# Heads in pairs on half-array tiles, and modulation slices in four column groups, in a two-layer diffusion trunk on Trainium2

## The chip, the cores and the metric

The program runs on one core of a Trainium2 chip. The metric is the device time of one execution in microseconds (us). The engines are PE (TensorE, matrix products), DVE (VectorE), ACT (ScalarE), POOL (GpSimd, here the indirect gathers) and SP (SyncE, which issues most DMAs). Each engine works off its own queue in a fixed order; semaphores tie the queues together.

## The reference

640 tokens (128 context tokens, group i; 512 latent tokens, group ii) of width 1024 pass two layers. A layer, cut to what matters here:

```python
sh1, sc1, g1, sh2, sc2, g2 = modulate(cvec, w_ada, b_ada)      # silu(c) @ w_ada + b_ada, 6 x 1024 per group
h = rmsnorm(x) * (1 + sc1) + sh1
qa, ka, va, ga, lrf, lrb, ch, cb, cc, qn, kn, vn = split_proj(h, w_in)
o_gla = gla_bidir(q, k, v, la_f, la_b, s0_f, s0_b)             # 6 heads of 64, both directions, chunked scan with decay
y_conv = cb * short_conv(cc * ch, conv_w, conv_b)              # 256 channels
o_na = neighbourhood_attention(qh, kh, vh, ...)                # 6 heads of 64, softmax(q k^T * scale + bias) v
x = x + g1 * (concat(y_gla, y_conv, o_na) @ w_out)
x = x + g2 * peer_ffn(rmsnorm(x) * (1 + sc2) + sh2, ...)       # product-key retrieval of 128 single-neuron experts
```

All products are float32 in result: the projections split each operand into a rounded part and its rest and add three products, the others are float32 matrix products as such.

## The kernel before

Channels lie on the 128 partitions, tokens along the free dimension (`T` = 640, five chunks of 128). Two heads of 64 channels share a partition block, so linear attention (GLA) and neighbourhood attention (NA) loop over three blocks `fc`, each a pair of heads: partitions 0 to 63 are one head, 64 to 127 the other.

**Modulation.** `w_ada` of a layer is 12 slices of 512 outputs, each 8 blocks of 128x512. `ada_steps` loads a block (256 KB, `wada`), multiplies it by the two conditioning columns `sc` (L160, `ps_ada`, 8 matmuls added up in one PSUM bank), copies the two rows out (L165, `arow`) and turns them to columns by four small matmuls (L172, `ps_at`). It is a generator: layer 0 takes slices 0 to 2 on PE and slice 3 on DVE (L158) ahead of everything else, slices 4 to 9 two blocks at a time between the head steps of its NA, and slices 10, 11 and layer 1's twelve during the retrieval front end of layer 0. Layer 1 computes none.

**Projections.** A chunk of 128 output channels (`proj`, L221) loads a 512 KB weight block, splits it (`whi` on ACT L217, `wlo` on DVE L218) and issues 48 matmuls (L233, `ps_pj`), 8 blocks of the width by 3 products by 2 halves of 320 tokens.

**GLA.** `pre(fc)` makes the decays (`dec`, a chain of `ps_z`, DVE `mz` and three ACT functions) and four projection chunks (192 matmuls): q, k, v, gate. `gla(fc)` computes the diagonal products `ps_d` (L339, contraction over one head's 64 partitions), and then seven levels of a doubling scheme: 20 records of `ps_lv` matmuls (L361; a float32 matmul leaves two records, and ten stand in a level), whose results go into `att` under a mask (L362, `copy_predicated`), after which `qz` (L375) and `kS` (L377) are scaled for the next level. `qz` is stored twice as wide, with zeros in the other head's half, so that one matmul over all 128 partitions gives both heads. A tail transposes `kS`, chains six state steps (`pk` L404 on PE, `st` L407 on DVE) and forms the output `po` (L419 from the states, L423 from `att`), which is normalised and gated. `pre(fc+1)` is emitted behind `gla(fc)`.

**NA.** `na(fc)` runs five query tiles for one head and then five for the other: scores `ps_s` (L506, L508), bias and row maximum on DVE (L511), exponential on ACT (L516), scaling on DVE (L518), transposes (L522, `pt`), a copy out (L524, `pT`), and the products with the values into 64 of 128 partitions (L527, `npo`). `napre(fc+1)` has three more projection chunks.

**Then** the output projection (8 chunks), and the retrieval layer: norm, query projections and top-k (`level1`, `select`), one-hot tables (`build`), then a loop over 128 rows of experts that holds PE, DVE, POOL and the DMA queues.

**Order.** The code emits instructions in program order, and a scheduler gives each engine one fixed order from it: work emitted later may be put ahead where the engine would otherwise stand idle by the scheduler's reckoning. So `pre(fc+1)`'s matmuls can stand between the levels of `gla(fc)`. What stands where is read from the order of the built program.

Of the kernel before, what the change touches and what calls it, by code (L numbers as in the profile page):

```python
# [42 lines left out]
CG = ((0, 1), (1, 5))  # L43
TG = 256
# [9 lines left out]
NADA = 2  # L54
# [4 lines left out]
ADAP = 3  # L59
ORDER = "b2 s3 b3 s4 l0 b4 s0".split()  # L60
BSEL = 16
ADA1 = 4
NWA = 4
# [6 lines left out]
class Trunk:  # L70
    def __init__(self, ctx, tc, I, O):
# [21 lines left out]
        self.sc = consts.tile([128, 8, 2], F32, name="sc")  # L93
        with tc.tile_pool(name="init", bufs=1) as ip:
            for name, shape, dst, dt in (("cT", [128, 8, 2], None, F32), ("lmask", [128, 7, 128], self.lmask, I32),
                                         ("thr", [128, 2, 16], self.thr, F32), ("nstep", [128, 16], self.nstep, F32),
                                         ("iota", [128, 128], self.iota, F32)):
                t = ip.tile(shape, dt, name="i_" + name)
                nc.scalar.dma_start(t, I[name])
                if dst is None:  # L100
                    S.activation(self.sc, t, AF.Silu)
                else:
                    V.tensor_copy(dst, t)
        self.eps = consts.tile([128, 1], F32, name="eps")
# [36 lines left out]
    def ada_steps(self, l, c0, c1, dve=False):  # L141
        nc, PE, S, V = self.nc, self.PE, self.S, self.V
        for m in range(c0, c1):
            pt = None
            if dve:
                part = self.wp.tile([128, 2, 512], F32, name="apart", tag="apart", bufs=1)
            else:
                ps = self.pss.tile([128, 512], F32, name="ps_ada", tag="s")
            for k in range(8):
                w = self.wp.tile([128, 512], F32, name="wada", tag="wadv" if dve else "wada", bufs=2 if dve else NWA)  # L150
                nc.sync.dma_start(w, self.I["w_ada"][l, m, k])
                if dve:
                    for g in range(2):
                        c = self.sc[:, k, g:g + 1]
                        if k == 0:
                            V.tensor_scalar(part[:, g, :], w, c, None, op0=OP.mult)
                        else:
                            V.scalar_tensor_tensor(part[:, g, :], w, c, part[:, g, :], op0=OP.mult, op1=OP.add)  # L158
                else:
                    PE.matmul(ps[0:2, :], self.sc[:, k, :], w, start=(k == 0), stop=(k == 7))  # L160
                if k < 7:
                    yield
            if not dve:
                row = self.adap.tile([2, 512], F32, name="arow", tag="arow")
                S.activation(row, ps[0:2, :], AF.Copy)  # L165
            pt = self.pss.tile([128, 4, 2], F32, name="ps_at", tag="s")
            for i in range(4):
                if dve:
                    for g in range(2):
                        PE.matmul(pt[:, i, g:g + 1], part[:, g, i * 128:(i + 1) * 128], self.one, start=True, stop=True)  # L170
                else:
                    PE.matmul(pt[:, i, :], row[:, i * 128:(i + 1) * 128], self.ident[0:2, 0:2], start=True, stop=True)  # L172
# [64 lines left out]
    def mix(self, l):  # L237
# [21 lines left out]
        first = chain.from_iterable(zip_longest(self.ada_steps(l, 0, ADAP), self.ada_steps(l, ADAP, 4, True))) if l == 0 else ()  # L259
# [23 lines left out]
        qz = [gp.tile([128, 2, T], F32, name=f"qz{d}") for d in range(2)]  # L283
        sts = [gp.tile([128, 4, 128], F32, name=f"st{d}") for d in range(2)]
        for d in range(2):
            for hh in range(2):
                r = slice(64 * hh, 64 * hh + 64)
                o = slice(64 - 64 * hh, 128 - 64 * hh)
                G.memset(qz[d][r, 1 - hh, :], 0.0)
# [32 lines left out]
        def gla(fc, X):  # L322
# [3 lines left out]
            for d in range(2):  # L326
                for hh in range(2):
                    r = slice(64 * hh, 64 * hh + 64)
                    V.tensor_tensor(qz[d][r, hh, :], q[r, :], dec[d][r, :], op=OP.mult)
            att = gp.tile([128, 5, 2, 128], F32, name="att", tag="att")  # L330
            PAIRS = ((0, 1), (1, 3), (3, 5))
            for c0, c1 in PAIRS:
                n = c1 - c0
                pd = [pss.tile([128, 2, 128], F32, name="ps_d", tag="s") for hh in range(2)]
                for hh in range(2):
                    r = slice(64 * hh, 64 * hh + 64)
                    for c in range(c0, c1):
                        cs = slice(c * 128, c * 128 + 128)
                        PE.matmul(pd[hh][:, c - c0, :], kS[0][r, cs], q[r, cs], start=True, stop=True)  # L339
                    V.scalar_tensor_tensor(att[:, c0:c1, hh, :], pd[hh][:, :n, :], 2.0,  # L340
                                           ident[:, None, :].to_broadcast([128, n, 128]), op0=OP.mult, op1=OP.mult)
            tot = dec
            for lb in range(7):
# [7 lines left out]

                for c0, c1 in PAIRS:
                    n = c1 - c0
                    ps = pss.tile([128, 2, 2, 128], F32, name="ps_lv", tag="s")
                    for c in range(c0, c1):
                        cs = slice(c * 128, c * 128 + 128)
                        for d in range(2):
                            z = 1 - d
                            o = ps[:, c - c0].rearrange("p h (n z b) -> p h n z b", z=2, b=b)[:, :, :, z, :]
                            x = qz[d][:, :, cs].rearrange("p h (n z b) -> p h n z b", z=2, b=b)[:, :, :, z, :]  # L360
                            PE.matmul(o, kS[d][:, cs], x, start=True, stop=True)  # L361
                    V.copy_predicated(att[:, c0:c1].rearrange("p c h t -> p (c h) t"),  # L362
                                      self.lmask[:, lb, None, :].to_broadcast([128, 2 * n, 128]),
                                      ps[:, :n].rearrange("p c h t -> p (c h) t"))
                nb = T // (2 * b)
                tv = [tot[d].rearrange("p (n z) -> p n z", z=2) for d in range(2)]
                for d in range(2):
                    z = 1 - d
                    qv = qz[d].rearrange("p h (n z b) -> p (h n) z b", z=2, b=b)[:, :, z, :]
                    if b == 1:  # L370
                        qv = qv[:, :, 0].rearrange("p (h n) -> p h n", h=2)
                        V.tensor_tensor(qv, qv, tv[d][:, None, :, d].to_broadcast([128, 2, nb]), op=OP.mult)
                    else:
                        qv = qv.rearrange("p (h n) b -> p h n b", h=2)
                        V.tensor_tensor(qv, qv, tv[d][:, None, :, d:d + 1].to_broadcast([128, 2, nb, b]), op=OP.mult)  # L375
# [34 lines left out]
            for g, (c0, c1) in enumerate(CG):  # L410
                n = c1 - c0
                po = pss.tile([128, 4, 128], F32, name="po", tag="s")
                for c in range(n):
                    cs = slice((c + c0) * 128, (c + c0 + 1) * 128)
                    first = True
                    if g:
                        for d in range(2):
                            for hh in range(2):
                                PE.matmul(po[:, c, :], qz[d][:, hh, cs], sts[d][:, c, :], start=first, stop=False)  # L419
                                first = False  # L420
                    for hh in range(2):
                        r = slice(64 * hh, 64 * hh + 64)
                        PE.matmul(po[:, c, r], att[:, c0 + c, hh, :], vt[:, c0 + c, r], start=not g,  # L423
# [61 lines left out]
        def na(fc, Y):  # L485
            q, k, vt = Y["q"], Y["k"], Y["vt"]
            po = [pss.tile([128, 4, 128], F32, name="npo", tag=f"o{i}", bufs=1) for i in range(2)]
            for hh in range(2):
                r = slice(64 * hh, 64 * hh + 64)
                bt = np_.tile([128, BW], F32, name="bt", tag="bt", bufs=2)  # L490
                nc.sync.dma_start(bt, I["bias"][l, 2 * fc + hh])
                for qt in range(5):
                    ps = pss.tile([128, 512], F32, name="ps_s", tag="s")
                    qs = slice(qt * 128, qt * 128 + 128)
                    s = np_.tile([128, 512], F32, name="ss", tag="ss", bufs=3)
                    mx = np_.tile([128, 4], F32, name="mx", tag="mx", bufs=4)
                    if qt == 0:
                        N = 128
                        PE.matmul(ps[:, :128], q[r, qs], k[r, :128], start=True, stop=True)
                        vs = [vt[:, 0, r]]  # L500
                        V.tensor_reduce(mx[:, 0:1], ps[:, :N], axis=AX.X, op=OP.max)
                        src = ps
                    else:
                        kt0, kn = NAK[qt - 1]
                        N = (kn + 1) * 128
                        PE.matmul(ps[:, :kn * 128], q[r, qs], k[r, (1 + kt0) * 128:(1 + kt0 + kn) * 128],  # L506
                                  start=True, stop=True)
                        PE.matmul(ps[:, kn * 128:N], q[r, qs], ck[r, fc, :], start=True, stop=True)  # L508
                        vs = [vt[:, 1 + kt0 + i, r] for i in range(kn)] + \
                             [cv[:, fc * 128 + 64 * hh:fc * 128 + 64 * hh + 64]]  # L510
                        V.tensor_tensor_reduce(out=s[:, :N], in0=ps[:, :N],  # L511
                                               in1=bt[:, BOFF[qt - 1][0]:BOFF[qt - 1][0] + N], scale=1.0,
# [7 lines left out]
                    nk = N // 128  # L520
                    for i in range(nk):
                        PE.transpose(pt[:, i, :], s[:, i * 128:(i + 1) * 128], ident)  # L522
                    pT = np_.tile([128, 4, 128], F32, name="pT", tag="pT", bufs=2)
                    S.activation(pT[:, :nk, :], pt[:, :nk, :], AF.Copy)  # L524
                    o = po[0][r, 0, :] if qt == 0 else po[1][r, qt - 1, :]
                    for i in range(nk):
# [43 lines left out]
    def peer(self, l):  # L570
# [55 lines left out]
        for h in range(PH):  # L626
# [10 lines left out]
            for _ in range(ADA1):  # L637
                next(ada, None)
# [369 lines left out]
```

## Time and profile before

| | us |
|---|---|
| median of 3 runs | 4127.65 (4120.05 to 4128.69) |
| the profiled execution | 4129.16, span 4127.4 |
| start to the first projection, layer 0 | 0 to 63 |
| GLA and one convolution, layer 0 / layer 1 | 113 to 316 / 2177 to 2380 |
| NA, layer 0 / layer 1 | 316 to 502 / 2380 to 2528 |
| output projection to the norm | 502 to 569 / 2528 to 2588 |
| retrieval front end to the row loop | 569 to 968 / 2588 to 2955 |
| row loop | 968 to 2094 / 2955 to 4088 |

The stages are read from the first instructions of each on PE. The profile is one execution; its own time is 1.5 us above the median of the runs. A table of windows gives the busy time of each engine in each stage and the granted PE clock, where 1.00 is 2.4 GHz and 0.50 is 1.2 GHz. A PE record is longer than the step from one to the next, since matmuls are pipelined: the step between starts is what counts.

### The profile page before, as it was taken

The page shows a single profiled execution, that of the slowest core. Times are in us where ns is not written, and L with a number is a line of the kernel's source. Part 1 is how long each engine was busy: PE and PEld are TensorE (multiplying, and loading weights), DVE is VectorE, ACT ScalarE, POOL GpSimd, SP SyncE. Part 2 cuts the span into 40 slices and gives each one's busy share as a digit, 9 for nine tenths or more (in the row PEclk, how much of TensorE's full clock was granted, in tenths as well). Part 3 has the DMA queues.
Part 4 walks back from the last instruction along what each step waited for, and adds up shares of the span by engine and source line. Part 5 has one row for each costly group of instructions (what it writes and reads, how often), then busy time and mean ns, then how long its engine had stood idle before and what let it go on. Part 6 is the DMA issues. An engine that isn't in the chain of part 4 may idle for free.

```text
span 4127.4 us, 53267 instructions
## 1 busy us (share of the span) xinstructions
PE 3806.6 (92%) x19884; PEld 3206.3 (78%) x19884; DVE 3336.6 (81%) x6619; ACT 1697.7 (41%) x3268; POOL 753.5 (18%) x532
## 2 busy tenths in 40 slices
PE   7999997888999999999989999857799999999998
PEld 4896775556888888888878988745588888888886
DVE  4762359878999999999967634888899999999997
ACT  4423331885333333333354242368633333333333
POOL 0000000002333333333300000000043333333331
PEclk8999998998999999999999999978899999999999
DMA  4114231667999999999921121113599999999995
GB/s 161 33 61 128 74 110 52 189 181 288 381 373 386 378 383 382 382 386 372 382 102 35 61 70 36 52 54 98 204 378 390 384 379 376 379 376 381 380 378 211
DMA packets 265394, 1011.80 MB, mean 245 GB/s; under 512 B 24176, under 2 KB 112624, under 8 KB 166576
## 3 DMA queue, kind: packets, MB, share of 16 engines
q0 software_dynamic: 73728, 536.90, 33.8%
q1 hardware_dynamic: 173696, 425.44, 27.9%
q10 hardware_dynamic: 17712, 46.07, 2.9%
q8 instruction: 156, 2.56, 0.2%
q14 instruction: 102, 0.84, 0.1%
HBM read 960.49 MB, written 47.84 MB: 244 GB/s over the span
## 4 chain that ended last, share of the span: by engine, by line
issue 34%; PE 33%; POOL 11%; ACT 9%; DVE 7%; DMA 6%; POOLq 0%; ACTq 0%; SPq 0%; DVEq 0%
PE ps_pj L233 13%; POOL uv L751 11%; DMA uv<-uv,gidx 5%; ACT qg L788 5%; PE acc L875 3%; PE ps_ada L160 3%; PE ps_lv L361 2%; PE ps_g L791 2%; PE npo L527 1%; ACT sg L799 1%; PE ps_ms L185 1%; PE ps_s L506 1%; PE ps_a L857 1%; PE ps_a L858 1%; PE ps_a L859 1%
## 5 line engine op out<-in xcount | busy, mean ns | idle before, releaser
L751 POOL DMA_INDIRECT uv<-uv,gidx x512 | 746.2, 1457 | 3304.4 <-DVE gacc L763 1366.3
L857 PE MATMUL ps_a<-hd,uhi 128*128 128x384 f32 x2048 | 698.5, 341 | 22.6 <-ACT uhi L836 22.6
L859 PE MATMUL ps_a<-hd,ulo 128*128 128x384 f32 x2048 | 693.0, 338 | 9.6 <-DVE ulo L837 9.4
L858 PE MATMUL ps_a<-hd,uhi 128*128 128x384 f32 x2048 | 692.1, 338 | 0.0
L754 DVE SCALAR_TENSOR_TENSOR uv<-uv,ht 128x1024 f32<-128x1024 f32 x512 | 623.5, 1220 | 84.4 <-DMA uv<-uv,gidx 83.6
L763 DVE SCALAR_TENSOR_TENSOR gacc<-uv,gw,gacc 128x1024 f32<-128x1024 f32 x508 | 652.5, 1284 | 16.1
L875 PE MATMUL acc<-vhi,whi 128*128 128x512 f32 x1536 | 506.3, 411 | 37.1 <-ACT whi L867 36.8
L875 PE MATMUL acc<-vhi,wlo 128*128 128x512 f32 x1536 | 484.5, 397 | 14.2 <-DVE wlo L868 13.8
L836 ACT ACTIVATE vhi<-raw 128x1024 fp32r<-128x1024 f32 x256 | 271.6, 1061 | 535.7 <-PE acc L875 526.6
L875 PE MATMUL acc<-vlo,whi 128*128 128x512 f32 x1536 | 479.7, 393 | 0.0
L857 PEld LDWEIGHTS ps_a<-hd,uhi 128*128 128x128 f32 x2048 | 386.4, 189 | 34.2 <-ACT uhi L836 24.0
L859 PEld LDWEIGHTS ps_a<-hd,ulo 128*128 128x128 f32 x2048 | 386.5, 189 | 15.4 <-DVE ulo L837 13.5
L858 PEld LDWEIGHTS ps_a<-hd,uhi 128*128 128x128 f32 x2048 | 386.5, 189 | 10.1
L875 PEld LDWEIGHTS acc<-vhi,whi 128*128 128x128 f32 x1536 | 271.2, 189 | 125.9 <-ACT whi L867 79.4
L788 ACT ACTIVATE qg<-ohq,gT 128x128 f32<-128x128 bf16 x768 | 341.3, 533 | 59.5 <-DVE ohq L784 59.5
L791 PE MATMUL ps_g<-ohp,qg 128*128 128x128 f32 x1536 | 295.9, 335 | 69.3 <-ACT qg L788 68.7
L875 PEld LDWEIGHTS acc<-vhi,wlo 128*128 128x128 f32 x1536 | 284.5, 189 | 91.6 <-DVE wlo L868 32.5
L791 PEld LDWEIGHTS ps_g<-ohp,qg 128*128 128x128 f32 x1536 | 236.3, 219 | 152.8 <-ACT qg L788 113.9
L875 PEld LDWEIGHTS acc<-vlo,whi 128*128 128x128 f32 x1536 | 290.3, 189 | 65.8
L837 DVE TENSOR_TENSOR vlo<-raw,vhi 128x1024 fp32r<-128x1024 f32 x256 | 312.1, 1219 | 12.6 <-ACT vhi L836 12.6
L837 DVE TENSOR_TENSOR ulo<-raw,uhi 128x1024 fp32r<-128x1024 f32 x256 | 312.4, 1220 | 1.7 <-ACT uhi L836 1.7
L756 ACT ACTIVATE gw<-dots 128x2 f32<-128x2 f32 x256 | 52.1, 203 | 615.4 <-DVE uv L754 615.2
(243 smaller groups left out, 6182.9 us busy)
## 6 DMA issues: line engine op xcount, KB each, us to landing
raw<-dn SPq DMA_DIRECT2D x256, 1024.0 KB
wada<-w_ada SPq DMA_DIRECT2D x192, 256.0 KB
gsp<-sg SPq DMA_DIRECT2D x48, 896.0 KB
gres<-gsp ACTq DMA_DIRECT2D x112, 384.0 KB
wraw<-w_in SPq DMA_DIRECT2D x56, 512.0 KB
wraw<-w_out SPq DMA_DIRECT2D x16, 512.0 KB
wraw<-wq SPq DMA_DIRECT2D x16, 512.0 KB
uv<-uv,gidx POOLq DMA_INDIRECT x512
```

Source lines behind the costliest of these rows:

```text
L233: self.PE.matmul(ps[j][:, :n], w[:, k, :], x[:, k, :], start=(k == 0 and i == 0), stop=(k == 7 and i == 2))
L751: G.indirect_dma_start(out=b, out_offset=None, in_=I["uv"], in_offset=bass.IndirectOffsetOnAxis(ap=gidx[t][:, s:s + 1], axis=0))
L754: V.scalar_tensor_tensor(b[:, :D], b[:, :D], 1.0, ht[t], op0=OP.mult, op1=OP.mult, accum_out=dots[:, s:s + 1])
L763: V.scalar_tensor_tensor(acc_, b[:, D:], w[:, s:s + 1], acc_, op0=OP.mult, op1=OP.add)
L788: S.activation(qg[:, t, :], ohq[:, :, t4 + t], AF.Copy, scale=gT[:, t0 + t4 + t:t0 + t4 + t + 1])
L791: PE.matmul(ps[:, t, :], qg[:, t, :], ohp[:, t4 + t, :], start=True, stop=True)
L836: S.activation(hi, raw, AF.Copy)
L837: V.tensor_tensor(lo, raw, hi.bitcast(F32), op=OP.subtract)
L857: PE.matmul(ps, uhi[:, ks], hd[0][:, k, :], start=(k == 0), stop=False)
L858: PE.matmul(ps, uhi[:, ks], hd[1][:, k, :], start=False, stop=False)
L859: PE.matmul(ps, ulo[:, ks], hd[0][:, k, :], start=False, stop=(k == 7))
L875: PE.matmul(acc[:, t, j, :], a[:, ts], x[:, j * 512:(j + 1) * 512], start=(b == 0 and i == 0), stop=(b == 127 and i == len(parts) - 1))
```

## The change

GLA and NA handle the two heads of a pair together. `qz` is no longer padded with zeros: a level is 20 matmuls of one head each (contraction over 64 partitions, 64 columns moving) instead of 10 over both, written alternately for partitions 0 to 63 and 64 to 127, into a bank for each head; the second head's bank is a single buffer (`o0`, `o1`). `copy_predicated` goes by head, `qz` and `kS` scalings cover 320 columns each, and the state product of `po` is one matmul per direction (L397) instead of two. In NA a query tile is taken for both heads before the next: two score banks, two softmax chains, and the value products alternate between output partitions 0 to 63 and 64 to 127. Modulation blocks come four at a time (1 MB, two buffers); four matmuls write 32 partitions each of one bank, whose copy covers all 128, and `sel` adds the four groups up in the `ps_at` matmuls. The conditioning columns `sc` are padded from 2 to 32. All slices go this way, slice 3 of the start too; the generator yields twice a slice instead of eight times.

```diff
+HR = (slice(0, 64), slice(64, 128))
...
+            ps = self.pss.tile([128, 512], F32, name="ps_ada", tag="s")
+            for h in range(2):
+                w = self.wp.tile([128, 4, 512], F32, name="wada", tag="wada", bufs=2)
+                nc.sync.dma_start(w, self.I["w_ada"][l, m, 4 * h:4 * h + 4].rearrange("k p n -> p k n"))
+                for i in range(4):
+                    PE.matmul(ps[32 * i:32 * i + 32, :], self.sc[:, 4 * h + i, :], w[:, i, :], start=not h, stop=bool(h))
...
+                PE.matmul(pt[:, i, :], row[:, i * 128:(i + 1) * 128], self.sel, start=True, stop=True)
...
-        first = chain.from_iterable(zip_longest(self.ada_steps(l, 0, ADAP), self.ada_steps(l, ADAP, 4, True))) if l == 0 else ()
+        first = self.ada_steps(l, 0, 4) if l == 0 else ()
...
-        qz = [gp.tile([128, 2, T], F32, name=f"qz{d}") for d in range(2)]
+        qz = [gp.tile([128, T], F32, name=f"qz{d}") for d in range(2)]
...
+            def banks(name, n):
+                return [pss.tile([128, 4, 128], F32, name=name, tag="s")[:, :n],
+                        pss.tile([128, 4, 128], F32, name=name, tag=f"o{int(n > 1)}", bufs=1)[:, :n]]
...
-                            PE.matmul(o, kS[d][:, cs], x, start=True, stop=True)
+                for c0, c1 in CG:
+                    n = c1 - c0
+                    ps = banks("ps_lv", n)
+                    for d in range(2):
+                        for c in range(c0, c1):
+                            cs = slice(c * 128, c * 128 + 128)
+                            for hh, r in enumerate(HR):
+                                PE.matmul((od, ev)[d](ps[hh][:, c - c0, :]), kS[d][r, cs], (od, ev)[d](qz[d][r, cs]),
+                                          start=True, stop=True)
+                    for hh in range(2):
+                        V.copy_predicated(att[:, hh, c0:c1, :], self.lmask[:, lb, None, :].to_broadcast([128, n, 128]),
+                                          ps[hh])
...
-                                PE.matmul(po[:, c, :], qz[d][:, hh, cs], sts[d][:, c, :], start=first, stop=False)
+                            PE.matmul(po[:, c, :], qz[d][:, cs], sts[d][:, c, :], start=not d, stop=False)
...
+                pss2 = [pss.tile([128, 512], F32, name="ps_s", tag="s") for hh in range(2)]
+                for hh, r in enumerate(HR):
+                    PE.matmul(pss2[hh][:, :kn * 128], q[r, qs], k[r, (1 + kt0) * 128:(1 + kt0 + kn) * 128],
+                              start=True, stop=True)
...
+                for i in range(nk):
+                    for hh, r in enumerate(HR):
+                        o = po[0][r, 0, :] if qt == 0 else po[1][r, qt - 1, :]
+                        v = vt[:, 1 + kt0 + i, r] if i < kn else cv[:, fc * 128 + 64 * hh:fc * 128 + 64 * hh + 64]
+                        PE.matmul(o, v, pTs[hh][:, i, :], start=(i == 0), stop=(i == nk - 1))
+                next(adas, None)
```

The order changes with it. First PE, layer 0, first GLA block, from the third level on (`ps_lv`: level products; `ps_pj`: projections of the next block). Before:

```order
L361 MATMUL ps_lv<-qz_420,kS_519 128x32x4 x3
L233 MATMUL ps_pj<-hhi,whi 128x320
L233 MATMUL ps_pj<-hlo,whi 128x320
L233 MATMUL ps_pj<-hhi,wlo 128x320
L361 MATMUL ps_lv<-qz_421,kS_706 128x32x4 x2
L361 MATMUL ps_lv<-qz_420,kS_519 128x32x4
L361 MATMUL ps_lv<-qz_421,kS_706 128x32x4 x2
L361 MATMUL ps_lv<-qz_420,kS_519 128x32x4
L361 MATMUL ps_lv<-qz_421,kS_706 128x32x4
L233 MATMUL ps_pj<-hhi,whi 128x320
```

Now, the same place, down to the first step of the tail:

```order
L345 MATMUL ps_lv<-qz_368,kS_463 128x16x4 x10
L345 MATMUL ps_lv<-qz_369,kS_650 128x16x4 x10
L345 MATMUL ps_lv<-qz_368,kS_463 128x8x8 x10
L345 MATMUL ps_lv<-qz_369,kS_650 128x8x8 x10
L345 MATMUL ps_lv<-qz_368,kS_463 128x4x16 x10
L345 MATMUL ps_lv<-qz_369,kS_650 128x4x16 x10
L345 MATMUL ps_lv<-qz_368,kS_463 128x2x32 x10
L345 MATMUL ps_lv<-qz_369,kS_650 128x2x32 x10
L345 MATMUL ps_lv<-qz_368,kS_463 128x64 x10
L345 MATMUL ps_lv<-qz_369,kS_650 128x64 x10
L266 MATMUL pt<-ident,kS_463 128x128 x5
L368 MATMUL pk<-vt,kt 128x128
```

No projection stands between the levels any more. Counted over the block, the 192 projections of the next one stood 84 in the levels, 49 in the tail and 59 behind `po`; now all 192 stand behind `po`. The second block of layer 0 and the first two of layer 1 read the same. In the third block, whose followers are the convolution and the first NA projections, 107, 64 and 147 `ps_pj` became 47, 42 and 208.

Second, PE in layer 0's NA, first block, around a query tile with four key blocks (`pt`: transposed scores, `npo`: products with the values, `ps_ada`: modulation). Before, one head:

```order
L522 MATMUL pt<-ident,ss 128x128 x4
L160 MATMUL ps_ada<-wada,sc 2x512
L527 MATMUL npo<-pT,nv 64x128 x3
L527 MATMUL npo<-pT,cv 64x128
L160 MATMUL ps_ada<-wada,sc 2x512
L506 MATMUL ps_s<-nk,nq 128x256
L508 MATMUL ps_s<-ck,nq 128x128
L160 MATMUL ps_ada<-wada,sc 2x512 x2
```

Now, both heads (ahead of these rows stand the first head's `pt` and one projection):

```order
L500 MATMUL pt<-ident,ss 128x128 x4
L151 MATMUL ps_ada<-wada,sc 32x512
L508 MATMUL npo<-pT,nv 64x128 x6
L508 MATMUL npo<-pT,cv 64x128 x2
L151 MATMUL ps_ada<-wada,sc 32x512 x3
L477 MATMUL ps_s<-nk,nq 128x384 x2
L481 MATMUL ps_s<-ck,nq 128x128 x2
L151 MATMUL ps_ada<-wada,sc 32x512 x4
```

A step now carries both heads: their value products stand in one run, and the scores of the next tile for both heads stand behind it; before, they were those of one head. The modulation comes in runs of four.

## Rows read from the trace of the kernel before

**Rows 1.** Windows by stage: us, busy (count) of PE, PEld, DVE, ACT, POOL, clock, DMA share, GB/s.

```profile
0.00:60.00 60.00, 43.53 (x117) 16.82 (x117) 21.24 (x33) 13.27 (x18) 3.72 (x12) 0.89 0.75 246
...
113.00:177.00 64.00, 61.37 (x452) 56.83 (x452) 49.77 (x103) 28.16 (x45) 0.00 (x0) 1.00 0.11 36
...
316.00:382.00 66.00, 65.94 (x332) 40.49 (x331) 17.66 (x55) 21.81 (x50) 0.00 (x0) 1.00 0.41 128
...
838.00:968.00 130.00, 104.02 (x497) 68.64 (x497) 102.71 (x337) 104.21 (x278) 4.92 (x4) 0.85 0.61 192
968.00:2094.00 1126.00, 1092.52 (x5361) 963.08 (x5362) 1054.08 (x1417) 400.51 (x638) 365.66 (x253) 0.99 0.95 373
```

**Rows 2.** The same view, layer 1: the first NA block, the front end.

```profile
2380.00:2429.00 49.00, 48.73 (x298) 39.92 (x298) 17.21 (x52) 20.87 (x51) 0.00 (x0) 1.00 0.22 74
...
2613.00:2943.00 330.00, 242.35 (x1193) 191.93 (x1192) 293.44 (x1188) 216.47 (x581) 0.00 (x0) 0.87 0.24 71
```

**Rows 3.** Timeline of the first GLA block, levels, DVE and PE: start, us, instruction.

```profile
116.48 0.43 DVE L362 COPY_PREDICATED att<-lmask,ps_lv 128x256 f32<-128x256 uint8 x1
...
139.53 0.31 PE L233 MATMUL ps_pj<-hhi,whi 128*128 128x320 f32 x1
...
140.07 0.81 DVE L375 TENSOR_TENSOR qz<-qz,tot 128x640 f32<-128x640 f32 x1
...
140.80 0.49 DVE L377 TENSOR_TENSOR kS<-kS,tot 128x320 f32<-128x320 f32 x1
...
141.20 0.82 DVE L375 TENSOR_TENSOR qz<-qz,tot 128x640 f32<-128x640 f32 x1
141.29 0.31 PE L233 MATMUL ps_pj<-hhi,whi 128*128 128x320 f32 x1
...
142.34 1.23 DVE L218 TENSOR_TENSOR wlo<-wraw,whi 128x1024 fp32r<-128x1024 f32 x1
...
142.62 1.72 PE L361 MATMUL ps_lv<-qz,kS 128*128 128x128 f32 x14
143.47 1.69 DVE L362 COPY_PREDICATED att<-lmask,ps_lv 128x256 f32<-128x256 uint8 x3
```

**Rows 4.** The same timeline at the block's start: the half-array products `ps_d`.

```profile
113.04 1.78 PE L339 MATMUL ps_d<-q,kS 64*128 64x128 f32 x20
```

**Rows 5.** The chain that ended last, 113 to 177: start, us, the state products.

```profile
161.37 0.90 PE po L419 x8
```

**Rows 6.** Timeline of PE at the start of the program: modulation and first projection.

```profile
20.70 4.69 PE L160 MATMUL ps_ada<-wada,sc 128*2 128x512 f32 x10
...
59.52 1.05 PE L172 MATMUL ps_at<-ident,arow 2*128 2x2 f32 x8 [0.74 <-ACT arow L165]
63.28 0.64 PE L233 MATMUL ps_pj<-hhi,whi 128*128 128x320 f32 x1 [2.71 <-ACT hhi L209]
```

**Rows 7.** Timeline of layer 1's NA, parts of the steps of one head.

```profile
2398.01 0.49 DVE L518 TENSOR_SCALAR ss<-ss,mx 128x512 f32<-128x512 f32 x1
...
2399.19 0.70 PE L506 MATMUL ps_s<-nk,nq 64*128 64x256 f32 x2
2399.36 0.60 ACT L524 ACTIVATE pT<-pt 128x512 f32<-128x512 f32 x1 [1.02 <-PE pt L522]
2399.73 0.38 PE L508 MATMUL ps_s<-ck,nq 64*128 64x128 f32 x2
...
2400.38 0.87 PE L527 MATMUL npo<-pT,nv 128*64 128x128 f32 x6
```

**Rows 8.** Groups of layer 1's NA, 2380 to 2528: count, busy us, mean ns, idle.

```profile
L516 ACT ACTIVATE ss<-ss,mx 128x512 f32<-128x512 f32 x12 | 8.7, 722 | 11.9 <-DVE mx L515 11.9
...
L511 DVE CUSTOM_DVE_ANT_0 ss<-ps_s,bt 128x512 f32<-128x512 f32 x12 | 8.3, 692 | 21.1 <-PE ps_s L508 21.1
```

**Rows 9.** Windows on PE in layer 1's table building: busy, clock, DMA.

```profile
2783.00:2789.80 6.80, 5.89 (x26) 0.75 0.46 135
2789.80:2796.60 6.80, 4.39 (x23) 1.00 0.25 73
```

More of the change, by code (lines that the diff above doesn't have):

```diff
@@ L1 @@
 from contextlib import ExitStack
-from itertools import chain, zip_longest
+from itertools import chain
 import numpy as np
@@ L53 @@
 NUV = 4
-NADA = 2
 UAFT = 2
@@ L100, in __init__ @@
                 if dst is None:
-                    S.activation(self.sc, t, AF.Silu)
+                    S.activation(self.sc[:, :, 0:2], t, AF.Silu)
                 else:
                     V.tensor_copy(dst, t)
+        V.tensor_copy(self.sel, self.ident[:, 0:2])
+        for j in range(1, 4):
+            V.tensor_tensor(self.sel, self.sel, self.ident[:, 32 * j:32 * j + 2], op=OP.add)
         self.eps = consts.tile([128, 1], F32, name="eps")
@@ L139, in run, with ada_steps @@
                 (self.nc.sync, self.nc.scalar)[k % 2].dma_start(self.O["yT"][k], t)
-    def ada_steps(self, l, c0, c1, dve=False):
+    def ada_steps(self, l, c0, c1):
         nc, PE, S, V = self.nc, self.PE, self.S, self.V
         for m in range(c0, c1):
[L144 to L161, printed above, removed]
@@ L166, in ada_steps @@
+            S.activation(row, ps, AF.Copy)
             pt = self.pss.tile([128, 4, 2], F32, name="ps_at", tag="s")
             for i in range(4):
[L168 to L172, printed above, removed]
+                PE.matmul(pt[:, i, :], row[:, i * 128:(i + 1) * 128], self.sel, start=True, stop=True)
@@ L503, in na @@
                     else:
[L504 to L510, printed above, removed]
                         V.tensor_tensor_reduce(out=s[:, :N], in0=ps[:, :N],
-                                               in1=bt[:, BOFF[qt - 1][0]:BOFF[qt - 1][0] + N], scale=1.0,
+                                               in1=bts[hh][:, BOFF[qt - 1][0]:BOFF[qt - 1][0] + N], scale=1.0,
                                                scalar=-3e38, op0=OP.add, op1=OP.max, accum_out=mx[:, 0:1])
@@ L636, in peer @@
                 level1([(t + i, h, qh[:, t + i - 1, :]) for i in range(2)])
-            for _ in range(ADA1):
-                next(ada, None)
+            next(ada, None)
         def select(t):
@@ L799, in build @@
                         S.activation(so, sp, AF.Copy)
-                for _ in range(NADA):
-                    next(ada, None)
+            next(ada, None)
             nc.sync.dma_start(gsp[:, :, tcn].rearrange("r p b t -> p r (b t)"), sg.rearrange("p r b t -> p r (b t)"))
```

94 lines of the change are left out of this document (34 added, 60 removed).

## Prediction

> **What bounds the kernel now.** I read the windows by stage first. The two row loops are 2259 of 4127 us [rows 1], by the table of stages; PE and DVE are both full there and none of their code changes, so everything lies in the other 1870 us. In GLA, PE is busy 61.4 of 64 us, DVE 49.8 [rows 1]; which of the two sets the pace is seen in the timeline of the levels [rows 3]: DVE goes from `copy_predicated` to `qz`, `kS`, `qz`, `kS`, one weight split and the next `copy_predicated` without a gap, while PE fills the rest of each level with projections of the next block. DVE sets the levels, and PE's spare time there is used. In layer 0's NA, PE is full, 65.9 of 66 us, and a block lasts 66 where layer 1's, without modulation, lasts 49 [rows 1, 2]. In the retrieval front end the clock is below 1 and PE not full [rows 1, 2]; layer 0 takes 399 us, layer 1 367 (table of stages).
>
> **Start.** Ten modulation records take 4.69 us [rows 6], 0.47 each, 0.94 a matmul of two records. Slices 0 to 3 run from 20.7 to 60.6 (the end of `ps_at`) [rows 6]. Now they come as eight halves of 1 MB. The window moved 246 GB/s at a DMA share of 0.75 [rows 1], so 328 GB/s if full, 3.2 us a half. Two halves wait at 20.7; six more take 19.2, with 2 for turn-around and 0.74 + 1.05 for the last slice's copy and `ps_at` [rows 6]: ready at about 44 to 45 if four column groups run together, **-15**. One after the other a half is 3.75 on PE: about 52, -9. At best -20.
>
> The trace has no column groups of different 32 columns next to each other, so their overlap is bounded from both sides, four times 0.94 and once. I take near the lower end, because two row halves do overlap here [rows 4] and the groups are independent in the same way.
> The Trainium skill (TensorE: Matmul & The Clock Gate, Measured speedup vs the span model) gives a speed-up of 2.38 for three column groups with 512 moving; no run here shows it, and by it four would be an estimated 1.6 us instead of 3.75 and the start -13.
>
> **GLA, four blocks followed by another.** This part loses, and it is read from the order: 84 projections stood in the levels, 49 in the tail, and now all 192 stand behind `po`. Projections step 0.147 us (twelve from 139.53 to 141.29 [rows 3]), so 133 x 0.147 = 19.6 us come out into the open, while DVE has nothing to do beside them.
> What comes back: a level lasted 5.40 (116.48 to 143.47, five levels [rows 3]). DVE's part was 1.69 for three copies, 2 x 0.73 for `qz`, 2 x 0.40 for `kS`; the rest, some 1.4, was weight splits, decays and `tot`. Now the same columns go in four copies, about 1.9, and `qz` covers 320 columns as `kS` does, 0.40: 1.9 + 1.6 = 3.5. Weight splits have moved behind `po` with their projections. A wait remains: the second head's bank is a single buffer, so its four matmuls wait for the last copy, and the reverse direction's ten stand behind them. At 0.11 a record (14 in 1.72 [rows 3]) and two at a time, that is about 0.9 + 1.1 us, of which DVE fills all but 0.4. Level: 4.0, saving 1.4; over the stretch about 7.5. If halves pair no better than `ps_d` did (20 records in 1.78, 0.089 [rows 4]; its order alternated only in part), the ten last 1.8 and a level 4.4: 16 us over all 42 levels. I count 6 of these 16.
> `po` loses half of its state products, 0.45 of 0.90 for each of four chunks [rows 5]: -1.8. Behind it 1.5 to 2 for the start of the projections (their first transposes wait for ACT, whose decay chain has moved there) and half a microsecond less in the tail.
> Sum for a block 19.6 - 7.5 - 1.8 + 2 - 0.5 = +12, **+48** for four; bounds +8 and +18 a block.
>
> **GLA, third blocks.** 171 projections under cover become 89: 82 x 0.147 = 12.1 come out, 5 come back in the levels, where some stay, and 1.8 in `po`: +5 each, **+10**. With the 6: GLA **+64**, bounds +42 and +96.
>
> **NA, layer 1.** Ten head steps share 49 us with 144 projections [rows 2]. Now five steps carry two heads, serially: the scores of both, 0.70 + 0.38 if they overlap as a pair [rows 7]; row maximum, 0.69 [rows 8], and its small follow-up; two exponentials, 2 x 0.72 plus their sum reads, about 1.8 [rows 8]; scaling 0.49 and transposes of the second head, 0.5; its copy out, 0.60 [rows 7]; eight value products, 1.2 if halves overlap, 2.3 if not (six records 0.87 [rows 7]). With some 0.1 at each of seven hand-overs this is 7 to 8 for four key blocks, a us less for three, about 4.7 for the context tile: 34 a block. About 95 of the 144 projections fit into the waits; 49 follow, 7 us. So 41 to 42 instead of 49, less in the next ones: **-14**, bounds -24 and 0.
>
> **NA, layer 0.** Six slices were 6 x (8 x 0.94 + 1.05) = 51 us on a full PE; they become 6 x (2 x 0.94 + 1.05) = 18, or 51 without overlap, and PE is no longer full. Its NA lasted 38 us more than layer 1's (186 and 148, table of stages); I leave 18 of this, and with layer 1's 14 this gives **-34**; without overlap of column groups -18, at best -46. The 1 MB loads hide: 12 MB in 150 us is under a third of what [rows 1] shows in the row loop.
>
> **Front end, layer 0.** Fourteen slices, 120 us of PE, become 41. They cost 32 us here (399 against 367), since PE was partly idle beside table building. In proportion 11 remain: **-18** with a little left for larger loads beside the table writes, -3 without overlap, -25 at best. POOL loses eight small clears of `qz` that lay beside the start: 0.
>
> **Sum.** -15 + 64 - 34 - 14 - 18 = -17. From the profiled execution, 4129.2, this gives 4112, and less the 1.5 by which it lies above the median, **4110**.
>
> **Rivals.** First, **PE's clock falls in GLA**, and the change ends slower. PE now waits in every level and in the tail. Table building, where PE works in short pieces with waits, shows what this can do: the clock is 0.75 and 1.00 in windows with 26 and 23 records, 0.87 over the stage [rows 9, 2]. At half clock the single-buffer loop of a level goes from 2.0 to 4.0 and the level from 4.0 to 5.5, 10.5 a block; `po` and the first projections add 5: +16 a block, 96 in all. At a quarter of the time, as in table building, it is +24: 4134; at two thirds +64: 4174. From 26% of the time on it is slower than before by more than can be told. Against it: the waits in a level are below 1 us, and in the first NA block of layer 1, chains of short steps too, the clock is 1.00 [rows 2].
> Second, **column groups don't overlap**: start -9, NA -18 and -8, front end -3, GLA as above: +26, 4154. For it: no row shows such an overlap. Against it: row halves do [rows 4].
> Third, **halves don't overlap in the levels** (the change doesn't do what it says): a level at 4.7 costs 29 instead of the 6 counted, and the scores of NA some 5 more: 4138. [rows 4] speaks against it.
> Fourth, **the gains come in full** (levels at 3.8, NA steps at 7, start -20, front end -25): GLA +42, NA -46 and -20: -69, 4059. For it: every link of these chains has its row; against it, that waits between engines add up.
>
> **How the numbers follow.** Chances: forecast, within 25 us of 4110, 0.50; clock 0.17; columns 0.11; halves 0.05; in full 0.17. A measurement of this kernel can tell about 0.2%, 8 us, from no change. Faster by more: 0.36 of the forecast's half, all of the last, 0.02 of the clock's: 0.55. Within: 0.13, and 0.05 of the rivals: 0.18. Slower: 0.01 + 0.15 + 0.07 + 0.04 = 0.27. The range, 4065 to 4165, leaves out the far end of the clock's case and of the last. The forecast alone would have 4085 to 4135.
>
> **What the new profile would show.** The first `ps_d` near 98 instead of 113. In layer 1's first GLA block, `copy_predicated` at a pace of 4.0, no `ps_pj` before `po`, then 192 in 28 to 30 us, and a `ps_d` period of 76 instead of 64: at 84 or more with a clock below 0.9 the first rival holds, at 79 with full clock the third. `ps_ada` in fours of about 1 us, or of 3.7: then the second. NA blocks of 41 to 43 in layer 1. Layer 0's front end within 15 us of layer 1's. I am wrong if GLA's period stays near 64, if the row loops change by more than a few us, or if NA, with serial steps, comes out longer than before.

## The result, and the profile after

| | us |
|---|---|
| before, median of 4 runs | 4125.69 (4120.05 to 4128.69) |
| changed, median of 4 runs | 4237.0 (4228.54 to 4240.44) |
| ratio | 1.0268, 95% interval 1.0248 to 1.0288 |
| the changed kernel's profiled execution | 4234.85, span 4233.1 |

The change costs 2.7%. Forecast were 4110 and a range from 4065 to 4165: wrong in sign and in size. Stages by the first instructions of each (a GLA block is counted from its `ps_d` to the next block's, the third to the first `ps_s`; NA with the output projection to the norm's first product on PE, `ps_ms`, which lies 9 us ahead of the boundary in the table of stages):

| stage | before | after | difference | forecast |
|---|---|---|---|---|
| start to the first `ps_d` | 113.0 | 103.0 | -10 | -15 |
| GLA, first two blocks, layer 0 and 1 | 127.8, 128.0 | 183.6, 183.7 | +111 | +48 |
| GLA, third blocks | 75.4, 75.4 | 109.9, 109.9 | +69 | +10 |
| NA to the norm, layer 0 | 243.5 | 195.6 | -48 | -34 |
| NA to the norm, layer 1 | 198.3 | 177.4 | -21 | -14 |
| norm to row loop, layer 0 | 408.1 | 408.2 | 0 | -18 |
| all else | | | +4 | 0 |

Within rounding these add up to the 105.7 us between the two spans (GLA's forecast has another 6 for pairing). NA gains more than forecast in both layers, the start less, the front end nothing; GLA loses 180 us where 64 were forecast.

Windows of the changed kernel, layer 0: length, busy us (instructions) of PE, PEld, DVE, ACT, POOL, granted clock, DMA share, GB/s. They are the first block's levels, its tail, its output products, the projections behind them, and the third block's levels.

```profile
103.00:144.00 41.00, 40.81 (x305) 38.63 (x304) 24.79 (x58) 1.36 (x2) 0.00 (x0) 0.55 0.04 14
144.00:158.00 14.00, 9.00 (x36) 6.46 (x35) 9.00 (x24) 9.95 (x18) 0.00 (x0) 0.62 0.02 5
158.00:163.00 5.00, 5.00 (x28) 5.00 (x29) 2.13 (x8) 2.88 (x5) 0.00 (x0) 0.60 0.04 10
163.00:194.50 31.50, 30.18 (x208) 29.52 (x207) 9.98 (x17) 14.94 (x22) 0.00 (x0) 1.00 0.15 52
...
286.60:348.00 61.40, 61.21 (x344) 54.02 (x345) 25.07 (x61) 2.87 (x4) 0.00 (x0) 0.54 0.03 9
```

The block of [rows 1] had DVE busy 49.8 of 64 us at clock 1.00. Now PE runs at half clock through most of levels, tail and output products, and gets its clock back only behind them, where the projections stand. Windows of 3 us at the start of these levels show the fall (length, busy us and instructions of PE, granted clock, DMA share, GB/s):

```profile
103.00:106.00 3.00, 3.00 (x42) 1.00 0.00 0
106.00:109.00 3.00, 2.81 (x21) 0.73 0.52 175
109.00:112.00 3.00, 3.00 (x13) 0.50 0.00 0
```

PE's records leave 0.19 us open in the first six us. Half-array products alone (`ps_d`, then `ps_lv`) stand there, so here it is not long waits of PE that come before the fall.

The timeline of DVE in the middle of the first block shows a level at half clock, as [rows 3] shows one before:

```profile
118.20 1.33 DVE L348 COPY_PREDICATED att<-lmask,ps_lv 128x512 f32<-128x512 uint8 x2 [0.43 <-PE ps_lv L345]
119.43 0.48 DVE L355 TENSOR_TENSOR qz<-qz,tot 128x320 f32<-128x320 f32 x1
119.82 0.49 DVE L357 TENSOR_TENSOR kS<-kS,tot 128x320 f32<-128x320 f32 x1
121.59 0.49 DVE L355 TENSOR_TENSOR qz<-qz,tot 128x320 f32<-128x320 f32 x1 [1.29 <-PE ps_lv L345]
122.00 0.49 DVE L348 COPY_PREDICATED att<-lmask,ps_lv 128x128 f32<-128x128 uint8 x2
122.40 0.48 DVE L357 TENSOR_TENSOR kS<-kS,tot 128x320 f32<-128x320 f32 x1
123.31 1.33 DVE L348 COPY_PREDICATED att<-lmask,ps_lv 128x512 f32<-128x512 uint8 x2 [0.43 <-PE ps_lv L345]
```

A level lasts 5.11 (118.20 to 123.31). DVE waits for PE twice in it, 1.29 and 0.43, 1.7 of the 5.1. Its own work is the 3.4 to 3.5 that the prediction put together. So this level is about as long as one with cover (5.40), and DVE now waits in it for a slow PE. The first two levels and the last are longer than before; their figures stand with the account of the prediction.

What went as forecast shows as plainly. The column groups overlap: in the timeline of the start, sixteen records (two halves of a slice, which need 7.5 us one after the other by [rows 6]) take 1.92, and once PE has waited for a load, eight take 1.94 at half clock (granted clock 0.50 from 30 to 55 us).

```profile
21.18 1.92 PE L151 MATMUL ps_ada<-wada,sc 128*32 128x512 f32 x16
23.82 1.05 PE L158 MATMUL ps_at<-sel,arow 128*128 128x2 f32 x8 [0.72 <-ACT arow L155]
27.85 1.94 PE L151 MATMUL ps_ada<-wada,sc 128*32 128x512 f32 x8 [2.97 <-DMA wada<-w_ada]
```

The Trainium skill (TensorE: Matmul & The Clock Gate, Measured speedup vs the span model) has 2.38 for three column groups; the rows above are nearer to four for four.

Layer 1's first NA block is 43 us (forecast 41 to 42, before 49 [rows 2]):

```profile
2506.00:2549.00 43.00, 42.89 (x296) 35.31 (x295) 16.98 (x60) 21.34 (x54) 0.00 (x0) 1.00 0.25 85
```

### The profile page after: what moved, and what is told of

It reads as the page before. It is cut to its first block, busy times and chain, and to the rows that moved or that the text cites. A ratio compares the mean times of both kernels' runs of the same rounds, so it can differ in the third digit from the quotient of the medians.

```text
span 4233.1 us, 54586 instructions
## 1 busy us (share of the span) xinstructions
PE 3877.1 (92%) x20636; PEld 3325.8 (79%) x20636; DVE 3291.1 (78%) x6626; ACT 1701.2 (40%) x3273; POOL 751.2 (18%) x524
## 4 chain that ended last, share of the span: by engine, by line
PE 34%; issue 33%; POOL 11%; DVE 8%; ACT 8%; DMA 5%; POOLq 0%; ACTq 0%; DVEq 0%
PE ps_pj L219 12%; POOL uv L730 11%; PE ps_lv L345 5%; DMA uv<-uv,gidx 4%; ACT qg L767 4%; PE ps_g L770 3%; PE acc L853 3%; PE ps_ada L151 2%; ACT sg L778 1%; PE ps_ms L171 1%; DVE i L599 1%; DVE i L603 1%; DVE s L597 1%; PE ps_a L837 1%; PE ps_a L835 1%
## 5 line engine op out<-in xcount | busy, mean ns | idle before, releaser
L770 PE MATMUL ps_g<-ohp,qg 128*128 128x128 f32 x1536 | 329.7, 353 | 85.0 <-ACT qg L767 83.7
L770 PEld LDWEIGHTS ps_g<-ohp,qg 128*128 128x128 f32 x1536 | 255.1, 228 | 187.9 <-ACT qg L767 142.9
L219 PE MATMUL ps_pj<-hhi,whi 128*128 128x320 f32 x896 | 291.6, 329 | 13.7 <-ACT hhi L195 10.7
```

The lines of the kernel that those rows point to most:

```text
L219: self.PE.matmul(ps[j][:, :n], w[:, k, :], x[:, k, :], start=(k == 0 and i == 0), stop=(k == 7 and i == 2))
L770: PE.matmul(ps[:, t, :], qg[:, t, :], ohp[:, t4 + t, :], start=True, stop=True)
```

## Experiments

Two theories were set against each other. **Theory 1:** the clock falls because PE has lost the projections that covered its waits in the levels. **Theory 2:** products on half the array hold the clock down, covered or not. Each total is set against the kernel before on the same chip. Where no interval is given, the kernel ran once; repeated runs of one kernel lie up to 19 us apart (4122.58 to 4141.96), so the stages in the traces weigh more there than the total.

**The cover taken from the kernel before.** Full-array levels, DVE work and bank use stay; `last` is the last output product, and `rest` holds the four projection chunks.

```diff
+            if last is None:
+                return rest(fc, X)
+            with tc.issue_after(last):
+                return rest(fc, X)
```

> The kernel before with one thing changed: in the first two GLA blocks of each layer the 192 projections of the next block stand behind the output products, as they do in the changed kernel; the levels stay full-array products over both heads. Theory 1 (the clock falls because PE now waits uncovered in the levels): granted clock 0.5 to 0.7 over the levels, a block of 85 to 92 us instead of 63.9, total 4210 to 4240. Theory 2 (the half-array products hold the clock down, covered or not): clock about 1.0 over the levels, a block of 76 to 80 (19.6 us of projections in the open, 5 to 7 back from levels without weight splits), total 4175 to 4190.

4238.8 against 4129.3 for the kernel before. The first two blocks last 91.5 and 92.8 us in layer 0 (91.5 and 92.1 in the changed kernel, 63.9 on average before): taking the cover away alone costs them what the whole change does. In the first block 19.4 of the 27.8 us stand behind the output products, where the projections are now in the open, and 8.4 come from slower levels, tail and output products. Windows of its first block's levels, tail and rest, then the second block's levels, columns as above:

```profile
115.10:154.20 39.10, 27.96 (x149) 23.99 (x148) 32.82 (x65) 13.02 (x15) 0.00 (x0) 0.79 0.05 14
154.20:170.00 15.80, 10.87 (x43) 9.27 (x43) 7.49 (x25) 4.25 (x11) 0.00 (x0) 0.50 0.02 5
170.00:204.90 34.90, 34.90 (x240) 34.26 (x239) 9.20 (x11) 9.62 (x17) 0.00 (x0) 0.97 0.15 47
206.60:247.70 41.10, 30.86 (x149) 27.14 (x148) 33.00 (x65) 13.02 (x15) 0.00 (x0) 0.67 0.04 14
```

Full-array levels without cover lose the clock too, to 0.79 and 0.67, with PE's records filling 28 of 39 us. Theory 2 alone falls. But with half-array products it is lower still, 0.55, and it falls there before PE has waited for long (2.81 of 3 us busy, above): waits are not the whole reason in the changed kernel, and shape seems to have a part. The two kernels also differ in banks, copies and DVE's work, so this isn't shape by itself.

**GLA alone undone in the changed kernel.** `gla` and the allocation of `qz` are those of before; paired NA and grouped modulation stay.

> The changed kernel with GLA alone undone: paired neighbourhood attention and four-group modulation stay. Both theories: GLA blocks back at 64 and 75 us with clock 1.0; start 10 us earlier than before, layer 0's NA to norm 48 us shorter, layer 1's 21 shorter, the front end of layer 0 as long as before: 4126 - 79 = 4047 (4038 to 4060). If the NA gain hung on what GLA left behind (clock, projections done early), it would be under half of this: above 4085.

4056.8, ratio 0.9817 (0.979 to 0.984), inside the expected 4038 to 4060. GLA blocks are back at 63.9 and 75.4; the start, layer 0's NA and layer 1's NA are 9, 46 and 19.5 us shorter than before. The loss is GLA's, and the rest of the change is a gain of 1.8%.

**Unread full-array products in the levels of the changed kernel**, sixteen and eight in each level. Their results go nowhere; they only give PE work.

```diff
+                    if n > 1:
+                        fl = self.psj.tile([128, 512], F32, name="fil", tag="j")
+                        for i in range(16):
+                            PE.matmul(fl[:, :320], self.identr, hhi[:, i % 8, :320], start=True, stop=True)
```

> The changed kernel with sixteen full-array matmuls of 320 columns added in each level, whose result nobody reads, so that PE waits less. Theory 1: clock back at 0.9 to 1.0 in the levels, a level of 4.3 to 4.8 instead of 5.1, total 4190 to 4215. Theory 2: clock stays at 0.5 to 0.6, a level of 9 to 10 us, total 4370 to 4420.

4181.3: more work on PE, and 56 us faster than the changed kernel, more than theory 1 expected (4190 to 4215). The first two blocks are 5 to 8 us shorter (83.4 to 86.6), the third ones 17 and 19 (92.4 and 91.1). From the third blocks' levels the 47 projections are gone as well, so not all of that gain is the clock's. Window of the first block's levels:

```profile
102.00:135.80 33.80, 33.61 (x381) 31.83 (x377) 24.43 (x55) 0.14 (x1) 0.00 (x0) 1.00 0.06 17
```

Half-array levels at clock 1.00: they can have it, with full-array products between them. A level lasts 4.9, longer than the 4.3 to 4.8 expected. In its timeline forty records of `ps_lv` take 2.45, 0.061 each; they pair fully, where `ps_d` before had 0.089 [rows 4]:

```profile
123.55 2.45 PE L345 MATMUL ps_lv<-qz,kS 64*128 64x64 f32 x40
```

> As the run with sixteen unread full-array matmuls in each level, with eight. If less filling still holds the clock (0.9 to 1.0), the levels get shorter than the 4.9 us of sixteen, 4.0 to 4.4, total 4150 to 4165. If eight are too little, clock 0.5 to 0.6, levels of 6 to 7.5, total 4250 to 4310.

4232.4, and neither of the two expectations as a whole. Windows of the levels of layer 0's first, second and third block, the same code three times:

```profile
106.60:157.00 50.40, 50.21 (x334) 44.85 (x330) 24.43 (x55) 0.10 (x1) 0.00 (x0) 0.54 0.04 11
...
210.40:240.10 29.70, 29.51 (x334) 26.35 (x330) 24.38 (x55) 0.12 (x1) 0.00 (x0) 1.00 0.06 19
...
289.10:318.90 29.80, 29.61 (x334) 26.45 (x331) 24.48 (x55) 0.16 (x1) 0.00 (x0) 1.00 0.06 19
```

In layer 1 all three were slow (49 to 51 us). The same instructions take 29.7 us at full clock or 50.4 at half, and with PE busy throughout in both. In the fast second block DVE's work is the same as in the changed kernel's levels (24.4 us of 29.7), and its levels, with eight products more on PE, last 4.1 to 4.4 from the second to the sixth, near the forecast's 4.0. That block lasts 78.7 in all, where the prediction has 76. So the arithmetic for a block was about right, and conditional on a clock which this code doesn't keep by itself. What tips a block to one side was not settled.

**Projections woven into the half-array levels by hand.** The next block's projections are a generator, stepped after each level and each state step: 66 in the levels, 63 in the tail, 63 behind, in the first two blocks of a layer.

```diff
+                for _ in range(2):
+                    next(wv, None)
...
+                        next(wv, None)
```

> The changed kernel with the next block's projections emitted between the levels and the tail's steps, so that 66 stand in the levels, 63 in the tail and 63 behind it (0, 0 and 192 in the changed kernel). Theory 1: clock 0.9 to 1.0 in the levels, a block of 64 to 68 us instead of 91.5, total 4130 to 4145. Theory 2: clock 0.5 to 0.6, a level of 8 to 9 us as in the third block, a block of 88 to 95, total 4225 to 4255.

4154.7, nearer to theory 1, with blocks of 68 and 71 us. Windows of the first and the third block's levels:

```profile
104.90:143.70 38.80, 38.60 (x359) 34.50 (x355) 30.20 (x72) 14.77 (x19) 0.00 (x0) 0.87 0.09 28
...
244.00:305.00 61.00, 60.81 (x332) 53.53 (x329) 24.55 (x59) 1.65 (x3) 0.00 (x0) 0.53 0.03 9
```

Cover brings most of the clock back, but the block is still no shorter than the 63.9 of before. PE's records fill both versions (38.6 of 38.8 here, at 0.87; 61.4 of 64 at 1.00 in [rows 1]), and a level's products take 2.45 in halves and about 2.4 over the full array (fourteen records in 1.72, six more at 0.11 [rows 3]). This leaves DVE's saving little room on PE; how long the woven block is at full clock throughout was not measured. The third block, which was not woven, stays at 61 us.

**Cover taken from the kernel before, and twelve unread products put in each level**, as many as projections stood there.

> The kernel before with the projections behind the output products (as in the first run) and twelve unread full-array matmuls in each level of the first two blocks, as many as projections stood there. Theory 1 (lost work on PE lowers the clock, and the clock is what costs beyond the 20 us in the open): clock of the levels back from 0.67 to 0.79 to 0.95 or more, levels of 35 us instead of 39 to 41, a block of 82 to 86 instead of 91.5, total 4200 to 4218. If the clock is not what lengthened the levels: 91 and 4235 to 4242.

4232.3: the expectation on the levels held, that on the total didn't. Windows of the first block's levels, and of its tail in two parts:

```profile
115.90:148.70 32.80, 31.96 (x232) 29.37 (x231) 28.32 (x51) 1.90 (x3) 0.00 (x0) 1.00 0.05 17
148.70:160.00 11.30, 7.51 (x31) 6.05 (x30) 8.29 (x22) 10.35 (x18) 0.00 (x0) 0.66 0.03 7
160.00:166.00 6.00, 1.18 (x5) 0.59 (x5) 4.18 (x16) 4.82 (x7) 0.00 (x0) 0.50 0.00 0
```

The levels are back at clock 1.00 and at 32.8 us instead of 39 to 41: work on PE sets the clock for full-array levels too. But with the filler the decay chain of the next block stands in the tail (ACT is busy 1.90 us in the levels instead of 13.02, DVE 28.32 instead of 32.82), so part of the 6 to 8 us may be the chain's. In the tail the state steps on DVE stand behind it: 17.5 us from the last level to the first state product, 13.6 without filler and 11.7 in the kernel before. The block is 88.4. So this run settles the clock in the levels, and not the price of the whole cover.

**No full-array products among the third block's levels.** In the changed kernel the first convolution and the first NA projections also go behind the output products.

> The changed kernel with the third block's followers (first convolution, first NA projections) also behind the output products, so that no full-array matmul stands among its half-array levels; 47 stood there. If mixing the two shapes at half clock is what made these levels 60.8 us long where the others take 39.9: levels of 40 us, the 47 come back behind at 0.15 each (7 us), a third block of 95 to 98 instead of 109.9, total 4205 to 4213. If the third block is long for another reason, 4228 to 4240.

4211.2, inside the range expected if the mixture is the reason. The third block of layer 0 lasts 98.4 instead of 109.9, its levels 35 instead of 61 (40 expected), still at clock 0.58. In the changed kernel's timeline of these levels (rows of PE and DVE, weight loads left out), projections and halves alternate at half clock:

```profile
305.36 0.47 PE L219 MATMUL ps_pj<-hhi,whi 128*128 128x320 f32 x1
305.62 0.47 PE L219 MATMUL ps_pj<-hlo,whi 128*128 128x320 f32 x1
305.89 0.47 PE L219 MATMUL ps_pj<-hhi,wlo 128*128 128x320 f32 x1
306.29 1.97 PE L345 MATMUL ps_lv<-qz,kS 64*128 64x64 f32 x8
308.18 0.63 PE L219 MATMUL ps_pj<-hhi,whi 128*128 128x320 f32 x1
308.29 0.49 DVE L355 TENSOR_TENSOR qz<-qz,tot 128x320 f32<-128x320 f32 x1 [3.56 <-PE ps_lv L345]
308.62 0.47 PE L219 MATMUL ps_pj<-hlo,whi 128*128 128x320 f32 x1
309.01 2.40 PE L345 MATMUL ps_lv<-qz,kS 64*128 64x64 f32 x20
```

A projection steps 0.26 to 0.27 at half clock, but 0.40 where halves follow (305.89 to 306.29) and 0.44 where it follows halves. And DVE waits 3.56 for products that stand behind projections which nobody waits for: cover that is slower than the hole it was put into.
The Trainium skill (TensorEngine Tiling (Array Packing), Key Properties) says that a change of tiling mode drains the engine; the steps of 0.40 and 0.44 instead of 0.27 agree.

**NA alone and modulation alone, in the kernel before.**

> The kernel before with the paired neighbourhood attention alone; GLA and modulation as before (a modulation slice still 8.5 us of PE). If the pairing gains by itself: layer 1's NA to norm 19 to 21 us shorter, layer 0's, where modulation keeps PE full, 12 to 25 shorter, total 4127 - 38 = 4089 (4080 to 4098). If the NA gain of layer 0 is modulation's alone: layer 0 unchanged, total 4104 to 4110.

4082.3, ratio 0.990 (0.988 to 0.993). Layer 1's NA to norm 19.5 shorter, layer 0's 20.7.

> The kernel before with the four-group modulation alone; GLA and NA as before. Start 9 to 10 us earlier, layer 0's NA 20 to 30 shorter (38 longer than layer 1's before, 18 of 51 us of PE left), the front end 0 to 8 longer: total 4127 - 31 = 4096 (4086 to 4106). If column groups brought nothing beyond the overlap seen at the start, NA of layer 0 would stay and the total be 4115 to 4122.

4091.4, ratio 0.993 (0.990 to 0.995). Start 10.6 earlier, layer 0's NA to norm 29 shorter, layer 1's the same. 20.7 + 29 = 50, against 48 together: in layer 0 the two gains add up, and each total lies inside its expectation. Both kernels ran twice.

**The best of both.** Paired NA, grouped modulation at the start and in NA, GLA of before, and in the front end the modulation of before.

> Paired neighbourhood attention, four-group modulation at the start and in layer 0's NA, GLA of the kernel before, and in layer 0's front end the modulation of the kernel before (256 KB blocks, one after the other). From the end of the norm to the end of layer 0's row loop the kernels with four-group modulation took 1530 to 1539 us, those with the old one 1517 to 1526. If the large blocks are what delays the loop: 12 to 20 us under the 4057 of the run with GLA undone, 4037 to 4045, and faster than all kernels so far. If that difference was the scatter of single executions: 4053 to 4061.

4044.4, ratio 0.980 (0.979 to 0.982) to before: 2% faster than the kernel before, 4.5% than the changed one (by the ratios), and inside the range expected for a delay by large blocks. From the norm to layer 1's it took 1544 us where the run with GLA undone took 1560, 14 of these 16 in the row loop itself; by the ratios (0.980 and 0.982, with intervals that overlap) the two kernels are not apart. Over all profiles layer 0's row loop takes 1131 to 1144 us with the small blocks in the front end and 1141 to 1154 with the large ones. So that large blocks delay the loop is not shown.

## Why the prediction was wrong

**What bounds GLA** was read from one side. [rows 1, 3] showed DVE without a gap, and PE busy 61.4 of 64. I took the first as the bound and the second as filling. By these figures both were near their bound: the same 192 projections and level products have to pass PE, and paired halves don't shorten them (2.45 against about 2.4 a level). With the cover left in place, a saving on DVE could have shortened the block by little more than the 2.6 us in which PE was idle. This is argued from the figures, and no run shows it at full clock.

**The projections in the open** were right: forecast 19.6 + 2 a block, measured 20.7 (31.5 behind the output products against 10.8).

**The levels** are the step that failed. The sum's term for them (4.0 a level instead of 5.40, -7.5 a block) had PE at full clock; measured are +4.6 (41.1 against 36.5 from `ps_d` to the last level's end) at clock 0.55. From one level's first product to the next's, levels three to six last 5.1 (5.1 to 5.7 before); the first two grew from 5.5 and 5.1 to 6.6 and 7.3, where the clock falls and the next block's decay products stand among the halves, and the last level's products take 5.6 instead of 2.8.

**The tail**: -0.5, measured +2.3 (14.0 against 11.7). **The output products**: -1.8, measured 0, since half the products at half clock take as long.

Together the three miss by 16.7 us a block (12.1, 2.8 and 1.8), and the first rival had priced a half clock at 16. By the prediction's own sign for it (a `ps_d` period of 84 or more with a clock below 0.9) this rival holds: the periods are 91.5 to 92.1. For the whole of GLA its 96 give 4206, against the measured 4237. The sum counted nothing for it and gave it a chance of 0.17, on two arguments that don't hold. That the waits in a level are below 1 us is no safeguard: the clock fell within six microseconds, with 0.19 us open between PE's records, and stayed low with 40.8 of 41 us filled. So the rival's own ground, that PE waits in every level, is not what the changed kernel's trace shows at the fall; it fits the run with full-array levels without cover. That NA kept 1.00 in [rows 2] was no evidence, since NA had projections between its steps. [rows 9], table building at 0.75 and 1.00 with short pieces of work, was a warning, but no row of the kernel before has half-array products in long runs by themselves.

That all three, levels, tail and output products, are the clock's rests on the windows; the block of 78.7 us, whose levels kept 1.00 with eight unread products each, is the nearest to a test. The bank of the second head, a single buffer, was not doubled in any run.

**The third blocks**: forecast +5 each, measured +34.5. Their 47 remaining projections were counted as cover. At half clock and between two shapes they lengthened the levels to 60.8, where the first block's, which have none, take 39.9; the run without them has 35 in the third block.

**Start**: -10 for -15. The groups overlap as the lower bound had it. PE waits for the loads, which was in the sum, and runs at half clock from the first of these waits on, which was not; a half comes every 3.6 us instead of 3.2.

**NA**: -48 and -21 for -34 and -14. The serial chain of a pair was right (43 for a block forecast at 41 to 42); later blocks gain more than I allowed. Layer 0 keeps 18 us over layer 1, as forecast, but had 45 over it before, counted to the norm, and not the 38 of the table's row for NA alone.

**Front end**: 0 for -18. By the sum PE was given back 79 us there, and the stage is as long as before. In table building PE, DVE and ACT are all at 103 to 104 of 130 us [rows 1], so nothing said that PE's share was what modulation cost; the proportion taken from 120 to 41 had no row behind it. The clock there is 0.84 (0.88 before, windows from the first table product to the last). In the runs with the modulation of before in this stage it takes 404 to 408 us, with the grouped one 405 to 412: its length doesn't hang on modulation's time on PE. What sets it was not tried.

The second and third rivals are out: columns overlap, halves overlap. The range ended at 4165, below even the two-thirds case of the first rival (4174), and its 16 a block left out what the third blocks pay.

## What to carry to other kernels

Before work is taken off an engine that never pauses, add up what the other full engine has to pass in the same stretch; if both are nearly full, a saving on one gains little. Then read from the new order what now stands in the old holes: work that filled waits on PE also held PE's clock here, and behind the loop it is paid twice, as time in the open and as half clock in the loop. Pairing half-array products pays where PE waits in a chain (NA) or is full of narrow products (modulation), with the rest of the stretch left as it was.

## What the runs showed of the hardware

- One code has two speeds: 29.7 us at 1.00 and 50.4 at 0.54 for the same levels, with PE's records without a pause in both. A PE that looks full isn't one that keeps its clock.
- Taking PE work away can cost time, and adding unread work can save it: sixteen unread products a level made the kernel 56 us faster, 27 us of it in the layers' first two blocks, where they displaced no projection from the levels.
- Two row halves in float32 run side by side at 0.061 us a record at full clock. Four column groups of 512 columns take the time of one: sixteen records in 1.92 us, where ten took 4.69 one after the other [rows 6].
